# First block, state bank and last rows: six small edits to a hybrid SSD and linear-attention layer

## The chip, the cores and the metric

The kernel runs on one core of one Trainium2 chip. The metric is the device time of one execution in microseconds (us); the median of three executions is compared.

## The reference, cut to what matters

One layer over 2048 real tokens and 16 meta tokens put in front of them, all in float32, width 1024:

```python
u = rmsnorm(hres, norm_w)
proj = jnp.einsum('bld,dn->bln', u, w_in)
z, xbc, dt_raw, q, k, v, g_gla, a_lr, merge_g = split_cols(proj, IN_WIDTHS)
# branch 1: conv + silu of xbc, state-space scan in chunks of 128; 16 heads in 4 groups
# branch 2: gated linear attention; log gates = log_sigmoid(a_lr @ w2 + b) / 16, summed along time; 4 heads
# both states start from the 16 meta tokens
branch_proj = jnp.einsum('blnc,ncd->blnd', branches, w_branch)
gates = jax.nn.sigmoid(merge_g.reshape(b, l, N_BRANCH, D_MODEL))
merged = jnp.sum(gates * branch_proj, axis=2)
return hres + jnp.einsum('bld,de->ble', merged, w_out)     # then a last rmsnorm; meta rows dropped
```

## The kernel before, in words

Each float32 operand of a large product is split into a high and a low half, and TensorE (PE) makes three products of the halves (`accum`, L214 to L216). ScalarE (ACT) makes the high half by a copy, VectorE (DVE) or GpSimd (POOL) the low half by a subtraction. For weights this is `load_w` (L175 on ACT, L177 on POOL) and `load_half` (L189, L190); the tile is `whl`, four buffers, its raw load `wr`, three.

The first part goes over four blocks of 512 tokens; block 0 also holds the meta tokens, and in the code `m0` is then 16, else 0. `load_u(b)` normalizes the block: per slice `kt` of 128 channels DVE scales (L342), ACT writes the high half (L345) and issues a store of the slice to memory (`u_left`, L346), DVE writes the low half (L347). For block 0 this happens at the very start, and the first product, `proj_zm`, goes through eight weight pieces `zm_0` to `zm_7`, in pairs, as the slices appear.

Within a block, generators are advanced by `step()`, once after each piece of the projections that PE works through; each `yield` is a step. The order on PE and on the queue of SyncE (SP) is the order of the code; on ACT, DVE and POOL a scheduler orders the instructions when the kernel is built, and each engine runs its list strictly in order. `gates(o)` makes the log gates of the four heads as two pairs: four small products (L488), each drained by DVE (L490) and ACT (L491), then Exp and Ln on ACT (L493, L494); the running sums (L498, L500, DVE) of each head are put off to the end of a step in block 0. Beside it `proj_conv` drains a projection on ACT (L593, L594), convolves on DVE (L598, three times), takes Tanh on ACT (L601), and `ssd_scan` works on one chunk a step (L662 to L700).

PSUM pools: `pj` (three banks) for projections, `pt` (three) for turns and small products, `pc` (two) for scans. In `gla_scan` of block 0 the state after the meta tokens is one product into a bank (L881), copied by DVE (L882), between products of `level_out` (L848) that use `pc`.

The second part (gates, two branches, output) runs as stages of products of sums (Strassen-Winograd); `sum_a(n)` makes three sums and a difference of an A operand on POOL, and `todo` holds at which position of the product order each step is written. The output stage scales finished rows: `use` takes the squares on ACT (L1251), POOL the power -1/2 (L1261, L1276), `finish` scales the two halves of a row (ACT L1283, DVE L1285 or L1287) and queues two stores, which go out from ACT's queue after the next product (L1377), or at the very end from SP's (L1432).

Of the kernel before, what the change touches and what calls it, by code (L numbers as in the profile page):

```python
# [43 lines left out]
def trunk_kernel(ctx: ExitStack, tc: tile.TileContext, xm, xmt, w_feat, w_tok, w_v3, w_zm, w_br, w_o,  # L44
                 cf32, cmsk, pvec, fnw, hvec, gw2, out):
    nc = tc.nc
# [85 lines left out]
    def bank(pool, tag):  # L132
        return mk(pool, [P, 512], F32, tag)
# [136 lines left out]
    def load_u(b):  # L270
        m0 = META if b == 0 else 0
        row0 = META - m0 + b * BLK
        tt = m0 + BLK
        u = []

        def rows_load(r0, n, i=None):
            xt = mk(wk, [P, D], F32, "tok4", bufs=NT4) if i is None else mk(spool, [P, META + BLK], F32, "acc")[:, :BLK]
            nc.sync.dma_start(xt[:n], xm[r0:r0 + n, :] if i is None else xm[r0:r0 + n, i * BLK:(i + 1) * BLK])
            return xt

        def rstd_rows(ss, n):
            r = mk(sm, [P, 1], F32, "rs1")
            nc.vector.tensor_scalar(r[:n], ss[:n], 1.0 / D, EPS, op0=ALU.mult, op1=ALU.add)
            done = nc.gpsimd.tensor_tensor(r[:n], r[:n], mhalf[:n, 0:1], op=ALU.pow)
            return (r, done) if m0 else r

        def rows_rstd(r0, n, vector):
            ss = mk(sm, [P, 1], F32, "ss")
            xt = rows_load(r0, n)
            if vector:  # L290
                nc.vector.scalar_tensor_tensor(xt[:n], xt[:n], 1.0, xt[:n], op0=ALU.mult, op1=ALU.mult,
                                               accum_out=ss[:n])
            else:
                nc.scalar.activation(xt[:n], xt[:n], AF.Square, accum_out=ss[:n])
            return rstd_rows(ss, n)

        rs = []
        if m0:
            rm_s = rows_rstd(0, META, True)
            for c in range(NCH):  # L300
                rs.append(rows_rstd(META + b * BLK + c * P, P, c % 2))
        else:
            for c in range(NCH):
                s2 = mk(sm, [P, 2], F32, "ss2")
                for i in range(2):
                    xt = rows_load(META + b * BLK + c * P, P, i)
                    nc.scalar.activation(xt, xt, AF.Square, accum_out=s2[:, i:i + 1])
                    if i == 0:
                        yield
                ss = mk(sm, [P, 1], F32, "ss")  # L310
                nc.vector.tensor_tensor(ss, s2[:, 0:1], s2[:, 1:2], op=ALU.add)
                rs.append(rstd_rows(ss, P))
                yield
        if m0:
            rs.append(rm_s)
            first_rows.append(rs[NCH - 1][1])
            rs = [r for r, _ in rs]
            nc.sync.dma_start(cst[:, :2], cf32[:, :2])
            nc.sync.dma_start(pv, pvec)
            for q in range(NWR):  # L320
                raws[f"zm_{q}"] = load_raw(w_zm[:, q * 288:(q + 1) * 288])
        rb = bank(pt, "pt")
        for c in range(NCH):
            nc.tensor.matmul(rb[:, c * P:(c + 1) * P], rs[c].to_broadcast([P, P]), ident, start=True, stop=True)
        rbs = [(rb, m0, BLK)]
        if m0:
            rm = bank(pt, "pt")
            nc.tensor.matmul(rm[:, :META], rs[NCH][:META].to_broadcast([META, P]), ident[:META, :META],
                             start=True, stop=True)
            rbs = [(rm, 0, META)] + rbs  # L330
        else:
            rbc = mk(spool, [P, 3 + META + BLK], F32, "cin")[:, :BLK]
            nc.scalar.activation(rbc, rb, AF.Copy)
            rbs = [(rbc, 0, BLK)]
            yield
        lows = []
        for kt in range(KT):
            xk = (mk(wk, [P, META + BLK], F32, "act", bufs=NACT) if m0 else mk(spool, [P, META + BLK], F32, "acc"))[:, :tt]
            nc.sync.dma_start(xk, xmt[:, kt, row0:row0 + tt])
            with tc.issue_after(lows[kt - 2].ins) if m0 and kt > 1 else nullcontext():  # L340
                for ps, a, n in rbs:
                    nc.vector.scalar_tensor_tensor(xk[:, a:a + n], xk[:, a:a + n], norm_w[:, kt:kt + 1], ps[:, :n],  # L342
                                                   op0=ALU.mult, op1=ALU.mult)
            u.append(u_tile(b)[:, :, :tt])
            nc.scalar.activation(u[kt][:, 0], xk, AF.Copy)  # L345
            nc.scalar.dma_start(u_left[b][kt], xk[:, m0:])  # L346
            lows.append(nc.vector.tensor_tensor(u[kt][:, 1], xk, u[kt][:, 0].bitcast(F32), op=ALU.subtract))  # L347
            if m0:
                first_low[:] = lows[:2][-1:]
            yield  # L350
        return u
# [116 lines left out]
    def gates(o):  # L468
# [12 lines left out]
        for h2 in range(0, GH, 2):  # L481
            gmt = mk(wk, [P, 2, META + BLK], F32, "tok4", bufs=NT4)
            for h in (h2, h2 + 1):
                gm = gmt[:, h % 2, :tt]
                gb = gate_b[:, h:h + 1]
                for i, (a, n) in enumerate(o.segs_all):
                    ps = bank(*((pj, "pj") if m0 and i == 0 else (pt, "pt")))
                    nc.tensor.matmul(ps[:, :n], w2[:, h * P:(h + 1) * P], ast[:, a:a + n],  # L488
                                     start=True, stop=True)
                    nc.vector.tensor_scalar(gm[:, a:a + n], ps[:, :n], gb, 0.0, op0=ALU.add, op1=ALU.min)  # L490
                    evicted[:] = [nc.scalar.activation(g_all[:, h, a:a + n], ps[:, :n], AF.Abs, bias=gb)]  # L491
            ga = g_all[:, h2:h2 + 2, :tt]
            nc.scalar.activation(ga, ga, AF.Exp, scale=-1.0)  # L493
            nc.scalar.activation(ga, ga, AF.Ln, bias=1.0)  # L494
            yield
            for h in (h2, h2 + 1):
                def sums(h=h):
                    nc.vector.tensor_tensor(gmt[:, h % 2, :tt], gmt[:, h % 2, :tt], g_all[:, h, :tt], op=ALU.subtract)  # L498
                    for a, n in chunks:
                        nc.vector.tensor_tensor_scan(g_all[:, h, a:a + n], ones[:, :n], gmt[:, h % 2, a:a + n], 0.0,  # L500
                                                     op0=ALU.mult, op1=ALU.add)

                if m0:
                    put_off.append(sums)
                else:
                    sums()
                yield


# [276 lines left out]
    def gla_scan(o, h, last=False):  # L786
# [90 lines left out]
        level_in(16)  # L877
        yield
        if m0:
            ps = bank(pc, "pc")  # L880
            nc.tensor.matmul(ps[:, :256], btm[:META], s_gla[:META, h], start=True, stop=True)  # L881
            nc.vector.tensor_copy(s_gla[:, h], ps[:, :256])  # L882
        level_out(32)
# [339 lines left out]
                         "p (k c) -> p k c", c=P), fetch, use)  # L1223

    def out_stage():
        fns, res, ssq, at_once = [], {}, {}, []

        def fetch(n, i, t):
            r0 = (2 * n + i) * P
# [7 lines left out]
        def use(n, i, t, ps, snap, cols=None):  # L1237
# [10 lines left out]
            c = cols or slice(0, BLK)  # L1248
            k = t + (c.start > 0)
            latest[:] = [nc.vector.scalar_tensor_tensor(r[:, c], ps[:, c], 0.5, r[:, c], op0=ALU.mult, op1=ALU.add)]  # L1250
            nc.scalar.activation(jk[:, c], r[:, c], AF.Square, accum_out=q[:, k:k + 1])  # L1251
            row = n, i, t
            if row == at_once[-1] or (first and (n, i) in [w[:2] for w in at_once[1:]]):
                if k < 2:
                    nc.vector.tensor_tensor(r[:, c], r[:, c], fns[t][:, c], op=ALU.mult)
                if k == 1 and not first:
                    mean(q)
                if k == 2:
                    last = nc.vector.scalar_tensor_tensor(q[:, 0:1], q[:, 2:3], 1.0 / D, q[:, 0:1],
                                                          op0=ALU.mult, op1=ALU.add)  # L1260
                    nc.gpsimd.tensor_tensor(q[:, 0:1], q[:, 0:1], mhalf[:, 0:1], op=ALU.pow)  # L1261
                    with tc.issue_after(last.ins):
                        nc.vector.tensor_tensor(r[:, c], r[:, c], fns[t][:, c], op=ALU.mult)
                    finish(*row)
            elif row in at_once:
                scale(*row)
                finish(*row)

        def mean(q):
            nc.vector.tensor_tensor(q[:, 0:1], q[:, 0:1], q[:, 1:2], op=ALU.add)  # L1270
# [63 lines left out]
        pos = max(pos, -1)  # L1334
        todo.setdefault(int(pos // 1), []).append((pos, fn))

    def load_sum_a(st, n):
        st.load_a(n)
        st.sum_a(n)

    for i, (st, n, p) in enumerate(order):
        if p == 1 and i >= NEARLY:
            at(i - LOAD + (n % 2), lambda st=st, n=n: load_sum_a(st, n))
    for si, st in enumerate(stages):
        for q in range(0 if si else 12, 28):
            p, j = PS[q // 4], q % 4
# [75 lines left out]
    for i, (st, n, p) in enumerate(order):  # L1422
# [5 lines left out]
            st.product(n, p)  # L1428
            flush(due)
        run(i)  # L1430
    for dst, src in stores:
        nc.sync.dma_start(dst, src)  # L1432
    run_out.close()


# [85 lines left out]
```

## Time and profile before

| what | value |
|---|---|
| three executions, us | 2244.68, 2245.72, 2250.13 (median 2245.72) |
| the profiled execution's own time, us | 2246.09 |
| its span (first to last instruction), us | 2244.0 |
| PE busy | 99% of the span |
| DVE, ACT, POOL busy | 70%, 53%, 31% |

Times in the profile's rows count from the start of the span; the profiled execution is 2.09 us longer than its span. A row of the timeline has the start, the length, the engine, line, operation, `out<-in` and a count (rows that follow each other are merged); in brackets stands how long the engine was idle before, and what ended that. ACTq and SPq are the queues' issues of transfers. A row of waits has engine and tile, what it waited for, and total, times and longest in us.

### The profile page before, as it was taken

What the parts mean: (1) busy time and instruction counts of PE and PEld (TensorE: products, weight loads), DVE (VectorE), ACT (ScalarE), POOL (GpSimd) and SP (SyncE); (2) the same over time, 40 slices, a digit from 0 to 9 for tenths busy, and PEclk for the clock granted to TensorE, in tenths of its full rate; (3) what the DMA queues carried; (4) which work ended last, traced back from release to release, by engine and by line L of the source; (5) the groups of instructions that cost most, each with busy time, mean ns of one, the idle gap of its engine ahead of it and who ended that gap; (6) DMA issues with size and microseconds to landing.
All of it is one profiled execution on the core that took longest, in us unless ns stands there. A gap on an engine that the chain in (4) does not pass through costs nothing.

```text
span 2244.0 us, 34943 instructions
## 1 busy us (share of the span) xinstructions
PE 2213.1 (99%) x11789; PEld 1896.7 (85%) x11789; DVE 1574.2 (70%) x2935; ACT 1188.8 (53%) x2767; POOL 688.1 (31%) x681
## 2 busy tenths in 40 slices
PE   7999999999999999999999999999999999999998
PEld 7999999888888888888988888878888888888887
DVE  5786676677657676557577666675678954789876
ACT  5666654476445456545465454454644545454544
POOL 4344433222222122221123100076233374324341
PEclk9999999999999999999999999999999999999999
DMA  8767876767778667778667664386768866677753
GB/s 310 237 226 237 267 257 213 220 207 248 240 250 267 205 215 236 240 250 268 208 219 226 212 216 157 125 260 200 242 220 292 303 221 216 239 281 249 254 178 123
DMA packets 314210, 517.94 MB, mean 231 GB/s; under 512 B 28080, under 2 KB 162480, under 8 KB 314032
## 3 DMA queue, kind: packets, MB, share of 16 engines
q1 hardware_dynamic: 246864, 419.63, 58.1%
q10 hardware_dynamic: 67168, 96.10, 11.8%
q8 instruction: 92, 1.51, 0.3%
q14 instruction: 86, 0.70, 0.1%
HBM read 368.42 MB, written 147.19 MB: 230 GB/s over the span
## 4 chain that ended last, share of the span: by engine, by line
PE 90%; DVE 3%; DMA 3%; ACT 2%; issue 1%; SPq 0%; POOL 0%; POOLq 0%; ACTq 0%; DVEq 0%
PE pj L214 20%; PE pj L216 20%; PE pj L215 20%; PE pt L214 4%; PE pt L215 4%; PE pt L216 4%; PE pc L687 2%; PE pc L214 2%; PE pc L216 2%; PE pc L215 2%; PE pc L848 2%; PE pc L688 1%; PE pc L690 1%; PE pc L956 1%; PE pt L662 1%
## 5 line engine op out<-in xcount | busy, mean ns | idle before, releaser
L214 PE MATMUL pj<-ue,whl 128*128 128x264 f32 (+1 forms) x672 | 236.3, 352 | 3.1 <-ACT g_all L491 2.2
L216 PE MATMUL pj<-ue,whl 128*128 128x264 f32 (+1 forms) x672 | 230.4, 343 | 0.0
L215 PE MATMUL pj<-ue,whl 128*128 128x264 f32 (+1 forms) x672 | 229.5, 342 | 0.0
L214 PE MATMUL pj<-uo,whl 128*128 128x512 f32 x512 | 205.7, 402 | 0.0
L216 PE MATMUL pj<-uo,whl 128*128 128x512 f32 x512 | 200.1, 391 | 0.0
L215 PE MATMUL pj<-uo,whl 128*128 128x512 f32 x512 | 199.4, 389 | 0.0
L215 PE MATMUL pj<-b,a 128*128 128x512 f32 (+1 forms) x484 | 188.0, 388 | 2.2 <-DVE b L1107 2.1
L214 PE MATMUL pj<-b,a 128*128 128x512 f32 (+1 forms) x484 | 188.7, 391 | 0.7 <-DVE io L1250 0.5
L216 PE MATMUL pj<-b,a 128*128 128x512 f32 (+1 forms) x484 | 188.9, 390 | 0.0
L598 DVE SCALAR_TENSOR_TENSOR acc<-cin,hcw,acc 128x512 f32<-128x512 f32 (+1 forms) x192 | 155.5, 810 | 41.6 <-ACT acc L594 40.3
L83 POOL TENSOR_TENSOR wr<-wr 128x256 f32<-128x256 f32 x80 | 67.9, 848 | 375.0 <-DMA wr<-y 160.1
L1132 DVE TENSOR_TENSOR a<-ar,a 128x512 fp32r<-128x512 f32 x160 | 132.8, 837 | 63.3 <-ACT a L1131 60.5
L1122 POOL TENSOR_TENSOR as<-ar,ar 128x512 f32<-128x512 f32 x40 | 63.0, 1575 | 370.3 <-DMA ar<-in_w_br 140.0
L1107 DVE TENSOR_TENSOR b<-br,b 128x512 fp32r<-128x512 f32 x140 | 128.7, 941 | 23.3 <-ACT b L1106 22.4
L214 PEld LDWEIGHTS pj<-ue,whl 128*128 128x128 f32 x672 | 127.0, 189 | 19.4 <-ACT g_all L491 2.4
L216 PEld LDWEIGHTS pj<-ue,whl 128*128 128x128 f32 x672 | 127.1, 189 | 14.9
L215 PEld LDWEIGHTS pj<-ue,whl 128*128 128x128 f32 x672 | 127.1, 189 | 14.7
L177 POOL TENSOR_TENSOR whl<-wr,whl 128x512 fp32r<-128x512 f32 (+1 forms) x76 | 97.8, 1294 | 131.0 <-ACT whl L175 73.6
L1132 DVE TENSOR_TENSOR a<-as,a 128x512 fp32r<-128x512 f32 x120 | 105.7, 882 | 42.5 <-ACT a L1131 39.8
L1166 ACT ACTIVATE sn<-pj 128x512 f32<-128x512 f32 x118 | 69.8, 592 | 122.6 <-PE pj L216 71.7
L1131 ACT ACTIVATE a<-ar 128x512 fp32r<-128x512 f32 x160 | 99.0, 624 | 56.4 <-PE pt L216 24.7
L215 PE MATMUL pt<-b,a 128*128 128x512 f32 x320 | 125.4, 392 | 0.1
(328 smaller groups left out, 6448.4 us busy)
## 6 DMA issues: line engine op xcount, KB each, us to landing
whl<-k_s SPq DMA_DIRECT2D x96, 512.0 KB, 3.7
whl<-k_g SPq DMA_DIRECT2D x96, 512.0 KB, 4.3
whl<-k_v SPq DMA_DIRECT2D x36, 512.0 KB, 4.0
wr<-in_w_feat SPq DMA_DIRECT2D x64, 256.0 KB, 4.5
k_s<-whl SPq DMA_DIRECT2D x32, 512.0 KB, 3.7
cb<-cumd SPq DMA_DIRECT2D x64, 256.0 KB, 5.0
y<-gg ACTq DMA_DIRECT2D x64, 256.0 KB, 4.0
k_g<-whl SPq DMA_DIRECT2D x32, 512.0 KB, 3.9
```

The lines of the kernel that those rows point to most:

```text
L83: nc.gpsimd.tensor_tensor(o, x, y, op=ALU.subtract)
L177: nc.gpsimd.tensor_tensor(hl[:, 1], raw, hl[:, 0].bitcast(F32), op=ALU.subtract)
L214: nc.tensor.matmul(ps, sh, mh, start=first, stop=False, **kw)
L215: nc.tensor.matmul(ps, sh, ml, start=False, stop=False, **kw)
L216: nc.tensor.matmul(ps, sl, mh, start=False, stop=last, **kw)
L598: convd[:] = [nc.vector.scalar_tensor_tensor(acc, cin[:, k:k + tt], hcw[:, ti, k:k + 1], acc, op0=ALU.mult, op1=ALU.add)]
L687: nc.tensor.matmul(py[:, h * 64:(h + 1) * 64], dm[:, h], xdt[:, h], start=True, stop=True)
L1107: nc.vector.tensor_tensor(t[:, 1], raw, t[:, 0].bitcast(F32), op=ALU.subtract)
L1122: nc.gpsimd.tensor_tensor(s1, a21, a22, op=ALU.add)
L1131: nc.scalar.activation(t[:, 0], src, AF.Copy)
L1132: latest[:] = [nc.vector.tensor_tensor(t[:, 1], src, t[:, 0].bitcast(F32), op=ALU.subtract)]
L1166: nc.scalar.activation(sn, self.ps[n, "a"], AF.Copy)
```

## The change

Six edits. (1) In block 0 the eight stores of `u_left` are issued from GpSimd's queue in place of ACT's. (2) In `gates` of block 0 one more `yield` follows the first pair of heads, so that the second pair's products come one step later. (3) The meta state of `gla_scan` takes a bank of `pt` in place of `pc`. (4) In the output stage, `finish` of the last row but one is called inside the last row's last `use`, behind its last square, and (5) the stores left at the end are reordered: the last row's later half goes from SP's queue ahead of its earlier half, which goes from ACT's. (6) `sum_a` is written three positions behind `load_a` for the first 28 positions.

```diff
-            nc.scalar.dma_start(u_left[b][kt], xk[:, m0:])
+            (nc.gpsimd if m0 else nc.scalar).dma_start(u_left[b][kt], xk[:, m0:])
...
                     sums()
                 yield
+            if m0 and not h2:
+                yield
...
         if m0:
-            ps = bank(pc, "pc")
+            ps = bank(pt, "pt")
             nc.tensor.matmul(ps[:, :256], btm[:META], s_gla[:META, h], start=True, stop=True)
...
-            nc.scalar.activation(jk[:, c], r[:, c], AF.Square, accum_out=q[:, k:k + 1])
+            squared = nc.scalar.activation(jk[:, c], r[:, c], AF.Square, accum_out=q[:, k:k + 1])
...
                 if k == 2:
+                    with tc.issue_after(squared.ins):
+                        finish(*unfinished.pop())
                     last = nc.vector.scalar_tensor_tensor(q[:, 0:1], q[:, 2:3], 1.0 / D, q[:, 0:1],
...
                 scale(*row)
-                finish(*row)
+                if row == at_once[-2]:
+                    unfinished.append(row)
+                else:
+                    finish(*row)
...
-            at(i - LOAD + (n % 2), lambda st=st, n=n: load_sum_a(st, n))
+            pos = i - LOAD + (n % 2)
+            at(pos, lambda st=st, n=n: st.load_a(n))
+            at(pos + (3 if i < 28 else 0), lambda st=st, n=n: st.sum_a(n))
...
-    for dst, src in stores:
-        nc.sync.dma_start(dst, src)
+    early, late = stores[-2:]
+    for (dst, src), q in zip(stores[:-2] + [late, early], [nc.sync] * (len(stores) - 1) + [nc.scalar]):
+        q.dma_start(dst, src)
```

**Edit 1, POOL at the start.** POOL's list before, from the third low half of the `zm` weights (`whl_443`) to the seventh (`whl_528`):

```order
L177 TENSOR_TENSOR whl_443<-wr_300,whl_443 128x288
L177 TENSOR_TENSOR whl_447<-wr_449,whl_447 128x288
L177 TENSOR_TENSOR whl_484<-wr_486,whl_484 128x288
L177 TENSOR_TENSOR whl_491<-wr_493,whl_491 128x288
L177 TENSOR_TENSOR whl_528<-wr_530,whl_528 128x288
```

And of the changed kernel, at the same place (`u_0` to `u_6` are the slices' stores):

```order
L177 TENSOR_TENSOR whl_443<-wr_300,whl_443 128x288
L346 DMA u_0_64<-act_309 128x512
L346 DMA u_1_65<-act_317 128x512
L346 DMA u_2_66<-act_325 128x512
L346 DMA u_3_67<-act_333 128x512
L346 DMA u_4_68<-act_341 128x512
L177 TENSOR_TENSOR whl_447<-wr_449,whl_447 128x288
L346 DMA u_5_69<-act_349 128x512
L177 TENSOR_TENSOR whl_484<-wr_486,whl_484 128x288
L346 DMA u_6_70<-act_357 128x512
L177 TENSOR_TENSOR whl_491<-wr_493,whl_491 128x288
```

Five stores now stand ahead of the fourth weight piece, and one between each of the next. On ACT the same stores stood between the high halves (L345) and are gone.

**Edit 2, PE at the second gate pair.** PE's list before, from the end of one convolution feature (`whl_1389`) to the start of the next (`whl_1492`):

```order
L216 MATMUL pj_1357<-ue_369,whl_1389 128x264
L488 MATMUL pj_1435<-act_1005,w_387 128x264
L488 MATMUL pt_1439<-act_1005,w_387 128x264
L488 MATMUL pj_1443<-act_1005,w_387 128x264
L488 MATMUL pt_1447<-act_1005,w_387 128x264
L662 MATMUL pt_1455<-cst,act_682 128x128
L662 MATMUL pt_1455<-cst,act_772 128x128
L662 MATMUL pt_1455<-cst,act_858 128x128
L687 MATMUL pc_1475<-c_161_1321,sq_1328 128x64 x4
L688 MATMUL pc_1475<-s_ssd,act_936 128x256
L690 MATMUL pc_1481<-c_162_1323,bt_1326 128x256
L214 MATMUL pj_1490<-ue_313,whl_1492 128x264
```

The changed kernel, from the same feature's end (its lines are two higher from there on: L664 is L662 of before):

```order
L216 MATMUL pj_1357<-ue_369,whl_1389 128x264
L664 MATMUL pt_1436<-cst,act_682 128x128
L664 MATMUL pt_1436<-cst,act_772 128x128
L664 MATMUL pt_1436<-cst,act_858 128x128
L689 MATMUL pc_1456<-c_161_1321,sq_1328 128x64 x4
L690 MATMUL pc_1456<-s_ssd,act_936 128x256
L692 MATMUL pc_1462<-c_162_1323,bt_1326 128x256
L214 MATMUL pj_1471<-ue_313,whl_1473 128x264
```

The four products L488 are gone from here; they stand behind the next feature, ahead of the next chunk. On ACT, the drains of that next feature (`pj_1471`) now stand behind the Tanh of the feature before it (`act_1431`; L603 and L595, L596 are L601 and L593, L594 of before):

```order
L679 ACTIVATE sq_1447<-sq_1447 128x512
L603 ACTIVATE act_1431<-acc_1421 128x528
L593 ACTIVATE cin_1874<-tails 128x3
L189 ACTIVATE whl_1690<-wr_1692 128x512
L595 ACTIVATE cin_1535<-pj_1471 128x264
L596 ACTIVATE acc_1536<-pj_1471,hcb,hcw 128x264
```

The drains keep their place behind that Tanh; what follows the feature on PE is now the second gate pair, and its third product takes the bank that this L596 leaves.

More of the change, by code (lines that the diff above doesn't have):

```diff
@@ L1225, in out_stage @@
     def out_stage():
-        fns, res, ssq, at_once = [], {}, {}, []
+        fns, res, ssq, at_once, unfinished = [], {}, {}, [], []
         def fetch(n, i, t):
@@ L1335, in at @@
         todo.setdefault(int(pos // 1), []).append((pos, fn))
-    def load_sum_a(st, n):
-        st.load_a(n)
-        st.sum_a(n)
     for i, (st, n, p) in enumerate(order):
         if p == 1 and i >= NEARLY:
-            at(i - LOAD + (n % 2), lambda st=st, n=n: load_sum_a(st, n))
+            pos = i - LOAD + (n % 2)
+            at(pos, lambda st=st, n=n: st.load_a(n))
+            at(pos + (3 if i < 28 else 0), lambda st=st, n=n: st.sum_a(n))
     for si, st in enumerate(stages):
```

## The prediction

> **What bounds the kernel now.** I read the page first, then who waited for whom on PE, then the timeline where those waits lie. The page:
>
> ```profile
> PE 2213.1 (99%) x11789; PEld 1896.7 (85%) x11789; DVE 1574.2 (70%) x2935; ACT 1188.8 (53%) x2767; POOL 688.1 (31%) x681
> ```
>
> PE bounds it. No product is added or taken away, so what the change can give is what PE loses in waits, and the tail behind its last product. PE's waits (total, times, longest):
>
> ```profile
> PE pt L324 <- DMA cst<-in_cf: 10.0, 1, 10.0
> PE pj L214 <- ACT ue L345: 2.4, 2, 1.5
> PE pj L214 <- ACT g_all L491: 2.2, 1, 2.2
> PE pc L848 <- DVE s_gla L882: 0.8, 1, 0.8
> PE pc L687 <- DVE sq L678: 0.8, 1, 0.8
> PE pj L488 <- ACT acc L594: 0.6, 1, 0.6
> PE pt L446 <- DVE ecu L443: 0.6, 1, 0.6
> PE pc L646 <- DVE c L698: 0.3, 1, 0.3
> PE pj L214 <- ACT alr L428: 0.2, 1, 0.2
> ```
>
> The first is the wait for the first rows, which no edit touches. All others that the edits touch come to some 7 us of 2244. A measurement of this kernel tells about 0.3%, 6.7 us, from no change; so the answer depends on small terms.
>
> **Edit 1, the start.** ACT's queue before:
>
> ```profile
> 12.90 1.55 DVE L342 SCALAR_TENSOR_TENSOR act<-act,pv,pt 128x512 f32<-128x512 f32 x3 [0.73 <-PE pt L324]
> 14.98 0.89 DVE L342 SCALAR_TENSOR_TENSOR act<-act,pv,pt 128x16 f32<-128x16 f32 x2
> 15.45 0.35 ACTq L346 DMA_DIRECT2D u<-act  x1
> 15.90 0.64 ACT L345 ACTIVATE ue<-act 128x528 fp32r<-128x528 f32 x1 [1.58 <-DVE act L342]
> 16.58 0.71 DVE L347 TENSOR_TENSOR ue<-act,ue 128x528 fp32r<-128x528 f32 x1 [0.71 <-ACT ue L345]
> 17.34 0.61 PE L216 MATMUL pj<-whl,ue 128*128 128x288 f32 x1
> ```
>
> DVE had scaled slice 1 at 12.90 + 1.55 = 14.45, yet ACT began its high half at 15.90: the store of slice 0 stood in front and got out only at 15.45. Without it ACT is done at 14.45 + 0.64 = 15.1. DVE then makes the low half right behind its next two scalings, at 14.98 + 0.89 = 15.87, and it is ready at 15.87 + 0.71 = 16.6, less the overlap that successive DVE rows show (0.1). PE's L216 of slice 1 goes at 16.5 in place of 17.34: 0.82 gained.
>
> The price lies on POOL, which makes the low halves of the weights:
>
> ```profile
> 11.59 2.29 POOL L177 TENSOR_TENSOR whl<-wr,whl 128x288 fp32r<-128x288 f32 x3
> 18.73 1.02 SPq L203 DMA_DIRECT2D wr<-in_w_zm  x1
> 21.27 1.33 POOL L177 TENSOR_TENSOR whl<-wr,whl 128x288 fp32r<-128x288 f32 x1 [7.38 <-DMA wr<-in_w_zm]
> 23.54 0.30 PE L215 MATMUL pj<-whl,ue 128*128 128x288 f32 x1
> 27.38 0.30 PE L215 MATMUL pj<-whl,ue 128*128 128x288 f32 x1
> ```
>
> POOL is free at 13.88, and PE first needs the fourth piece's low half (the row at 21.27) at 23.54, by my gain at 22.7. Five stores stand in between. If one costs x on POOL, the piece is ready at 13.88 + 5x + 1.33, in time while x is below 1.5. No trace of before has a DMA on POOL. The nearest rows are an issue on ACT (0.35) and SP (1.02) and a POOL instruction (1.33); I take 1.1, between the latter two and nearer to the issue, which is the same kind of work. The stores wait for their slices too: at a scaling and a low half a slice (0.89 + 0.71) slice 4 comes from DVE at 14.98 + 2 x 1.6 + 0.89 = 19.1, so the fifth store ends at 20.2 and the piece is ready at 21.5, in time. The later stores stand one between two pieces, where POOL waits for ACT's high half; that wait hides them. A gain on POOL is excluded, since it only gets work.
>
> [...] No run here shows a POOL DMA yet.
>
> ACT, freed of eight issues, also runs ahead later. The copy that frees the bank (L428) moves ahead of a weight split, and so does the head of the dt chain, which had stood behind this one:
>
> ```profile
> 38.01 0.63 ACT L175 ACTIVATE whl<-wr 128x512 fp32r<-128x512 f32 x1 [2.29 <-DMA k_s<-whl]
> ```
>
> That takes away the waits of 0.2 (alr) and 0.6 (ecu). Start: 0.8 + 0.2 + 0.6 = 1.6 gained.
>
> **Edit 2, the second gate pair.** Before:
>
> ```profile
> 90.62 0.47 PE L214 MATMUL pj<-ue,whl 128*128 128x264 f32 x1
> 95.80 0.65 ACT L601 ACTIVATE act<-acc 128x528 f32<-128x528 f32 x1 [2.69 <-DVE acc L598]
> 96.72 0.39 PE L488 MATMUL pj<-act,w 48*128 48x264 f32 x1
> 97.24 0.56 ACT L594 ACTIVATE acc<-pj,hcb,hcw 128x264 f32<-128x264 f32 x1
> 97.85 0.39 PE L488 MATMUL pj<-act,w 48*128 48x264 f32 x1 [0.62 <-ACT acc L594]
> 97.86 3.98 DVE L500 TENSOR_TENSOR_SCAN g_all<-ones_r,tok 128x16 f32<-128x16 f32 x5
> 100.24 0.47 PE L214 MATMUL pj<-ue,whl 128*128 128x264 f32 x1
> 103.13 0.39 PE L214 MATMUL pj<-ue,whl 128*128 128x264 f32 x1 [2.16 <-ACT g_all L491]
> 103.68 0.75 DVE L598 SCALAR_TENSOR_TENSOR acc<-cin,hcw,acc 128x528 f32<-128x528 f32 x1
> 107.02 0.76 DVE L598 SCALAR_TENSOR_TENSOR acc<-cin,hcw,acc 128x528 f32<-128x528 f32 x1
> 104.40:107.70 3.30, 3.30 (x18) 3.30 (x17) 3.30 (x10) 3.28 (x10) 0.00 (x0) 0.52 0.18 50
> ```
>
> DVE's running sums of the first pair (to 101.84) hold the drains of the second pair; PE waits 2.16, and then, the last row says, runs 3.3 us at a granted clock of 0.52, another 3.3 x 0.48 = 1.6 lost. Now the pair comes a feature later. That feature starts without the four products, 97.85 to 100.24 less their own half us, at 98.7, and takes what the one before took, 90.62 to 96.72: the pair's first product is due at 104.8, the third at 105.3. The third needs the bank that ACT drains (L594), and on ACT that stands behind Tanh L601 of the feature before. That one waits for DVE's convolution, which stands behind the same running sums: free at about 102.1, nine instructions that took 103.68 to 107.78 before, done at 106.2. From L601 to the first L594 ACT took 95.80 to 97.80, 2.0 us: the bank is free at 108.2. So the stall does not go, it moves: 2.9 us on L488, for 0.6 + 2.2 before. Behind the third product the rest is as before (2.4 us), so the z projection starts at 110.6 and not, as before, 1.5 us later, clock loss included; if the low clock comes again (the longer stall makes that likely) 1.5 - 1.6 = -0.1. The waits on L678 (0.8) and L698 (0.3) go, since the Ln and the sums leave that step. Edit 2: 1.0 gained, 2.6 without low clock.
>
> [...]
>
> **The rest.** Edit 3 takes the state's copy off the two `pc` banks, so the next products no longer wait for it: the 0.8 goes. A bank of `pt` is one more in use of three; its last reader there is a copy on ACT that ended while PE ran the projection in between, so it costs nothing; were that cover gone, the wait would be again at most the copy's own 0.8. Edit 6 does not do what it says: no row of any engine's list moves by it, POOL's four sums stand where they stood, so it is nothing. Edits 4 and 5, the tail:
>
> ```profile
> 2237.07 0.72 ACT L1283 ACTIVATE io<-io,ssf 128x512 f32<-128x512 f32 x1 [1.18 <-POOL ssf L1276]
> 2237.26 0.74 DVE L1287 SCALAR_TENSOR_TENSOR io<-io,ssf,br 128x512 f32<-128x512 f32 x1
> 2237.70 0.40 ACT L1251 ACTIVATE junk<-io 128x256 bf16<-128x256 f32 x1
> 2238.23 0.16 DVE L1259 SCALAR_TENSOR_TENSOR ssf<-ssf 128x1 f32<-128x1 f32 x1 [0.22 <-ACT junk L1251]
> 2239.91 0.82 SPq L1432 DMA_DIRECT2D out_h<-io  x2
> ```
>
> The last square no longer stands behind a scaling of 0.72; it could go 0.3 earlier, but DVE's next step stays behind L1287, which ends at 2238.0: 0.2. Of two stores one after the other on SP (0.82) each queue has one: 0.4. The row before's two stores, now ahead of the last on SP, are issued before it is due. Tail: 0.6.
>
> Sum: 1.6 + 1.0 + 0.8 + 0.6 = 4.0 us. Against the profiled execution's own 2246.09 that is 2242.1; the median of the runs shown lies 0.4 lower, so I forecast 2241.7 for the median.
>
> **The rivals.** *The stall goes altogether.* The sums' 3.98 us are long: ten of the same took 2.79 later, five 1.4. Two of POOL's splits (L190) ran beside the long ones:
>
> ```profile
> 123.59 2.79 DVE L500 TENSOR_TENSOR_SCAN g_all<-ones_r,tok 128x16 f32<-128x16 f32 x10
> ```
>
> If the second split falls behind the sums (on ACT its high half now stands behind L675), DVE is 2.6 us earlier, the new stall is 0.3, and 0.6 + 2.2 + 1.6 + 0.8 + 0.3 less 0.3 = 5.2 are won in place of 1.0: 8.2 in all, 2237.5. Against it: another split, that of the piece before, stays beside the sums. Chance 0.24.
>
> *POOL's stores cost more*; this one ends slower than before. If each store takes a POOL instruction's 1.33 and is held by the DVE pair beside it (0.89), x is 2.22: the fourth piece is ready at 13.88 + 11.1 + 1.33 = 26.3, 3.6 late; two more stores and pieces (2 x 3.55) later the sixth comes at 33.4, and PE, which needed it at 27.38, wants it at 27.38 - 0.8 + 3.6 = 30.2: 3.2 more. The start pays 6.8 against its gain of 1.6; with the other edits' 2.4 that is 6.8 - 1.6 - 2.4 = 2.8 slower, 2248.5. It decides from x = 1.5. For it: the same subtraction took 1.33 with DVE at work, and 2.29 for three of them without much of it. Chance 0.12, a third of it past 0.3%, for an x nearer to 3. [...]
>
> *The start's lead is eaten.* From 20 to 40 us the DMA engines are full:
>
> ```profile
> 20.00:40.00 20.00, 19.76 (x147) 19.55 (x146) 10.23 (x24) 9.89 (x26) 8.97 (x8) 1.00 0.97 330
> ```
>
> If the weights' loads pace PE as soon as it is earlier, the 1.6 go and 2.4 stay: 2243.3. Against it: no wait of PE there names a weight. Chance 0.16.
>
> **How the numbers follow.** The forecast itself has 0.48. Its own bounds are 2240.1 (no low clock) and 2243.3. The range takes in the first rival and the third and stops short of the second's 2248.5: 2236.5 to 2247.0; less than 0.2 is left out. Faster by over 0.3% (below 2239.0) is the first rival and 0.02 of the forecast's edge: 0.26. Slower by that (above 2252.4): 0.04. The rest, 0.70, is within.
>
> **What would show it.** Right: L216 of slice 1 near 16.5; POOL's DMA rows near 1.1 us and no wait of PE on a `whl`; PE's wait on g_all gone, one of 2 to 3 us on L488 behind L596, with a clock row near 0.5 behind it; no wait on s_gla; the last two issues side by side, 0.6 earlier. Wrong: a wait on L177, or no wait at all at the second pair.

## The result

The changed kernel takes 2243.57 us (median of 21 runs, 2239.68 to 2246.45), the kernel before 2246.85 (21 runs, 2244.68 to 2251.68): a ratio of 0.9984, 95% interval 0.9978 to 0.9990. It is faster by 3.3 us by the medians, 2.2 to 4.9 by the interval. Forecast were 2241.7 and a gain of 4.0, in a range of 2236.5 to 2247.0.

The changed kernel's profiled execution took 2246.45, the longest of its 21, with a span of 2244.7. So the two spans can't be subtracted; I compare stretch by stretch. PE runs the same 11,789 products, so the start of one product, counted from PE's first, says how far ahead PE is there. The page's row of PE, then PE's waits (total, times, longest):

```profile
PE 2211.9 (99%) x11789; PEld 1896.8 (85%) x11789; DVE 1577.0 (70%) x2935; ACT 1187.0 (53%) x2767; POOL 693.9 (31%) x689
PE pt L215 <- DVE b L1109: 3.9, 3, 1.7
PE pj L488 <- ACT acc L596: 3.1, 1, 3.1
PE pc L214 <- DVE c L946: 1.9, 4, 0.6
PE pj L214 <- ACT ue L345: 1.5, 1, 1.5
PE pj L214 <- ACT acc L596: 1.2, 2, 1.1
PE pt L446 <- DVE ecu L443: 1.0, 1, 1.0
PE pj L214 <- ACT alr L428: 0.6, 1, 0.6
```

Gone are the waits on s_gla, g_all, sq, tok and the c of L698, and that on ecu at 41.7 us (the 1.0 here lies at 768). New are 3.1 on L488, as forecast, and 1.1 on acc, which was not. The wait on alr, which was to go, grew from 0.2 to 0.6. The 3.9 on b lies at 1477 to 1484, far from any edit.

The start, POOL's queue and the product of slice 1 on PE:

```profile
14.07 1.35 POOL L346 DMA_DIRECT2D u<-act  x2
16.28 0.54 POOL L346 DMA_DIRECT2D u<-act  x1 [0.86 <-DVE act L342]
20.24 0.80 POOL L177 TENSOR_TENSOR whl<-wr,whl 128x288 fp32r<-128x288 f32 x1 [0.26 <-ACT whl L175]
20.98 0.56 POOL L346 DMA_DIRECT2D u<-act  x1
16.65 0.61 PE L216 MATMUL pj<-whl,ue 128*128 128x288 f32 x1 [0.33 <-DVE ue L347]
```

L216 goes at 16.65 where it went at 17.34. The first two stores take POOL 1.35 together, each later one 0.54 to 0.56, and the fourth piece is ready at 21.04.

The second gate pair, stretches of 3.4 us (length, busy time and count of PE, PEld, DVE, ACT, POOL, then PE's granted clock, DMA share, GB/s):

```profile
103.20:106.60 3.40, 1.24 (x9) 0.88 (x7) 3.40 (x8) 1.23 (x4) 0.00 (x0) 0.99 0.61 202
106.60:110.00 3.40, 2.42 (x11) 2.19 (x11) 3.39 (x7) 3.40 (x10) 2.85 (x3) 0.50 0.07 26
110.00:113.40 3.40, 3.40 (x13) 3.04 (x13) 3.23 (x8) 3.40 (x10) 1.24 (x2) 0.50 0.97 317
113.40:116.80 3.40, 3.40 (x31) 3.40 (x30) 3.04 (x6) 2.78 (x5) 0.00 (x0) 1.00 0.41 125
```

PE stands still, then has half its clock (0.50) for two such stretches; DVE is full through the first two. That row of DVE, not PE's, is the one to read here.

The last stores: issues in the timeline, then the issues of the last few stores with their time to landing (us at the end of the row), of the changed kernel and, last row, of the kernel before:

```profile
2239.29 1.31 SPq L1438 DMA_DIRECT2D out_h<-io  x3
2240.37 0.34 ACTq L1438 DMA_DIRECT2D out_h<-io  x1
out_h<-io SPq DMA_DIRECT2D x1, 256.0 KB, 2.5
out_h<-io ACTq DMA_DIRECT2D x1, 256.0 KB, 3.0
...
out_h<-io SPq DMA_DIRECT2D x1, 256.0 KB, 2.3
```

The table shows how far ahead (minus) or behind PE is at the same product, against the kernel before's profile, at times of that profile. "ch." is the changed kernel.

| kernel | 20 us | 52 | 60 | 96 | 140 | 400 | 425 | 1450 | 2236 |
|---|---|---|---|---|---|---|---|---|---|
| ch. | -0.80 | -1.75 | -0.88 | -0.82 | -1.70 | -2.38 | -3.46 | -1.12 | +0.58 |
| ch. again | -0.97 | -3.17 | -2.39 | -2.01 | -4.00 | -4.72 | -5.69 | -3.94 | -4.51 |
| edit 1 alone | -0.99 | -1.19 | -0.41 | -0.40 | -0.51 | -0.72 | -0.94 | -0.37 | 0.00 |
| edit 2 alone | -0.58 | -0.74 | -0.72 | -0.70 | -2.63 | -2.87 | -3.08 | -3.13 | -2.62 |
| ch. without 2 | -0.80 | -2.22 | -1.44 | -1.10 | -1.14 | -1.70 | -2.78 | -2.60 | -3.21 |
| edits 3 to 6 | -0.52 | -0.35 | -0.36 | -0.03 | +2.07 | +1.39 | +0.31 | +1.19 | +0.36 |
| ch. without 5 | -1.00 | -3.55 | -2.55 | -2.55 | -3.66 | -4.32 | -5.40 | -2.13 | -0.58 |
| ch., 48-row filler | -0.80 | -2.19 | -1.41 | -1.41 | -1.83 | -2.33 | -3.41 | -1.10 | -1.22 |
| ch., split moved | -0.81 | -2.73 | -2.47 | -2.47 | -2.90 | -3.64 | -4.72 | -3.46 | -3.35 |
| ch., two steps | -0.81 | -2.74 | -1.95 | -1.24 | -4.43 | -5.22 | -6.35 | -4.93 | -5.68 |
| ch., 128-row filler | -0.80 | -2.34 | -1.56 | -0.93 | -2.64 | -3.32 | -4.40 | -2.68 | -0.94 |
| two steps, split, old tail | -0.80 | -2.21 | -1.96 | -1.38 | +0.08 | -0.67 | -1.80 | -0.98 | -0.03 |
| the same, three steps | -0.81 | -2.78 | -2.44 | -1.51 | -0.69 | +1.92 | +0.84 | +2.22 | +2.12 |

A single row is one execution, and where no edit is, executions of like kernels differ by up to 3 us (the columns 425 and 1450); what a column does in all rows with an edit, and in none without, is the edit's.

### The profile page after: what moved, and what is told of

It reads as the page before. It is cut to its first block, busy times and chain, and to the rows that moved or that the text cites. A ratio compares the mean times of both kernels' runs of the same rounds, so it can differ in the third digit from the quotient of the medians.

```text
span 2244.7 us, 34971 instructions
## 1 busy us (share of the span) xinstructions
PE 2211.9 (99%) x11789; PEld 1896.8 (85%) x11789; DVE 1577.0 (70%) x2935; ACT 1187.0 (53%) x2767; POOL 693.9 (31%) x689
## 3 DMA queue, kind: packets, MB, share of 16 engines
q8 instruction: 92, 1.51, 0.3%
## 4 chain that ended last, share of the span: by engine, by line
PE 89%; DVE 4%; DMA 3%; ACT 2%; issue 1%; POOL 1%; SPq 0%; POOLq 0%; ACTq 0%; DVEq 0%
PE pj L214 20%; PE pj L216 20%; PE pj L215 19%; PE pt L215 4%; PE pt L214 4%; PE pt L216 4%; PE pc L689 2%; PE pc L214 2%; PE pc L216 2%; PE pc L215 2%; PE pc L850 2%; PE pc L690 1%; DMA acc<-in_xmt 1%; PE pc L692 1%; PE pc L958 1%
## 5 line engine op out<-in xcount | busy, mean ns | idle before, releaser
L216 PE MATMUL pj<-ue,whl 128*128 128x264 f32 (+1 forms) x672 | 229.7, 342 | 0.0
L216 PE MATMUL pj<-uo,whl 128*128 128x512 f32 x512 | 200.1, 391 | 0.0
L216 PE MATMUL pj<-b,a 128*128 128x512 f32 (+1 forms) x484 | 188.9, 390 | 0.3 <-DVE a L1134 0.3
L216 PEld LDWEIGHTS pj<-ue,whl 128*128 128x128 f32 x672 | 126.4, 188 | 14.9
```

The source lines that it names most:

```text
L216: nc.tensor.matmul(ps, sl, mh, start=False, stop=last, **kw)
```

## The experiments

The experiments ran in three groups of four, each beside its own 33 runs of the kernel before (medians 2246.21, 2245.85 and 2246.04). A ratio is against those, so kernels of different groups are compared by their ratios.

**The edits one by one.** Edit 1 alone:

```diff
-            nc.scalar.dma_start(u_left[b][kt], xk[:, m0:])
+            (nc.gpsimd if m0 else nc.scalar).dma_start(u_left[b][kt], xk[:, m0:])
```

> The kernel before with edit 1 alone (u's left stores from GpSimd's queue). I measure how much earlier PE does the same product than in the kernel before, counted from PE's first product. Theory (the start's lead is won at once and half of it is spent by 56 us): 0.8 us earlier at 20 us, 1.1 at 28, 1.6 behind the wait on ecu (45 us), then a wait of about 1.1 us on acc at 55, which leaves 0.9 at 60; nothing of the later waits moves, so the whole run is 0.9 us shorter. Rival A: the wait on acc at 55 us belongs to edit 2 and not to this one; then 1.6 to 1.75 stay at 60 and to the end. Rival B (POOL's stores cost): a wait on a whl low half (L177) between 20 and 30 us and less than 0.3 left at 45.

Measured: 2244.73 against 2246.21 for before, ratio 0.9990 (0.9981 to 0.9999). PE's wait on acc is there (1.0), so it belongs to edit 1: rival A falls. The lead grew to 1.59 at 28 us but was lost to weight pieces between 30 and 32 us (0.9 behind ACT's high half of whl and 0.5 behind POOL's low half, after 0.3 behind another low half at 22), a part of rival B. POOL's issues are not the cause: ACT itself waited 3.59 for the load of the piece at 30 us, 1.34 for the same one in the changed kernel's profile, and no other profile with edit 1 has those waits. So in this execution the weights came late. That is the rival "the start's lead is eaten", in one execution of eleven.

Edit 2 alone:

```diff
+            if m0 and not h2:
+                yield
```

> The kernel before with edit 2 alone (one step more between the two gate pairs). Theory: the waits of 0.6 at 97.85 and 2.2 at 103.13 go, one of 3.1 us on L488 at about 108 comes, with a clock row at half speed behind it for about 6.8 us in place of 3.4; the waits on sq, c and tok between 118 and 130 (0.8, 0.3, 0.2) go; together PE is 0.9 us earlier at 140 us than in the kernel before, and the run 0.9 us shorter. Rival (the low clock's length is chance, not a result of where the stall lies): the stall as said, but 3.4 us of half clock, and 2.4 or more earlier at 140 us. Rival (the start's lead of edit 1 is what removes the waits between 118 and 130): those waits stay, and PE is 0.4 us later at 140 than before.

Measured: 2245.41, ratio 0.9994 (0.9985 to 1.0003). From 96 to 140 us PE gains 1.93, with one stretch of half clock of 3.4 us; the waits on sq, c and tok are gone without the start's lead, so they go by edit 2 and the last rival falls. The length of the half clock differs from one execution to the next, as the first rival says (6.8 and 3.4 us in the two profiles of the changed kernel), though the gain stayed below its 2.4. PE's waits of this kernel and, second pair of rows, of edit 1 alone:

```profile
PE pj L488 <- ACT acc L596: 3.2, 1, 3.2
PE pc L850 <- DVE s_gla L884: 0.6, 1, 0.6
...
PE pj L214 <- ACT g_all L491: 2.1, 1, 2.1
PE pc L687 <- DVE sq L678: 2.0, 1, 2.0
```

The second pair matters. In this execution without edit 2 PE stood 2.1 us at g_all and no half clock followed, yet PE came out no earlier: the wait on sq, 0.8 in the profile before, was 2.0.

The changed kernel without edit 2:

```diff
-            if m0 and not h2:
-                yield
```

> The changed kernel without edit 2. Theory: PE keeps the 0.9 us that the start leaves at 60 us through 140 us, with the waits of 0.6 and 2.2 us at the second gate pair back and 3.4 us of half clock; state bank 0.8 to 1.1 at 425; tail nothing; in all 1.7 to 2.0 us shorter than before, that is 0.9 us slower than the changed kernel. Rival (the parts don't add): with the start's lead but without the step the stall on g_all grows by what the lead gave, and at 140 us nothing is left: 0.8 to 1.1 shorter than before in all.

Measured: 2243.56, ratio 0.9989 (0.9981 to 0.9998). From 96 to 140 us it gains 0.04; the waits are 0.6, 2.1 and 2.0, with no half clock. The start and the bank are won, as the theory says, and the stall on g_all did not grow. By time it is no slower than the changed kernel: 0.9 us is less than these medians tell.

Edits 3 to 6, that is the changed kernel without those two lines and with

```diff
-            (nc.gpsimd if m0 else nc.scalar).dma_start(u_left[b][kt], xk[:, m0:])
+            nc.scalar.dma_start(u_left[b][kt], xk[:, m0:])
```

> The kernel before with edits 3 to 6 (state bank, tail, sums) and neither 1 nor 2. Theory: no difference up to 300 us; the wait on s_gla at 421.75 gone, 0.8 us earlier behind it; the tail from PE's last wait (2235.20 before) to the last landing as long as before (7.4 us; the pair of queues gives nothing, since the store on ACT's queue lands 3.0 us after its issue beside three on SP's where it took 2.1 before): 0.8 us shorter in all. Rival (my forecast): the tail is 0.6 us shorter, 1.4 in all. For the waits on b between 1470 and 1492 (2.1 us in the profile before, 4.2 in the changed one): if edits 3 to 6 make them, they are near 4 here; if they vary from one execution to the next, anything from 2 to 4.

Measured: 2245.83, ratio 0.9996 (0.9987 to 1.0005). The wait on s_gla is gone and PE gains 1.08 between 400 and 425 us; with nothing changed there, edits 1 and 2 alone show 0.2. The tail from PE's last wait to the last landing is 7.48 us, as the theory says and not as I forecast. The waits on b were 2.0. From 96 to 140 us, where this kernel has no edit, PE loses 2.1 in this execution: it waits 2.0 on sq, and the clock is halved for 6.8 us behind it.

**The tail.** The changed kernel without edit 5:

```diff
-    early, late = stores[-2:]
-    for (dst, src), q in zip(stores[:-2] + [late, early], [nc.sync] * (len(stores) - 1) + [nc.scalar]):
-        q.dma_start(dst, src)
+    for dst, src in stores:
+        nc.sync.dma_start(dst, src)
```

> The changed kernel without edit 5: the last stores all on SP in their old order, edit 4 kept. The tail is counted from PE's last wait (L214 behind io, 2235.20 before, 2235.91 changed) to the last landing: 7.41 us before, 7.48 changed. Theory (edit 4 wins 0.25 and the store on ACT's queue, which takes 3.0 us to land where SP's took 2.3, gives it back): 7.15 to 7.25 here, the whole 0.25 us shorter than the changed kernel. Rival (the stores of the row before, which edit 4 puts behind the last square, crowd the last ones on SP's queue): 7.5 or more, since now all four stand on one queue. My forecast's terms would make it 7.4 less 0.2 here and 0.4 more in the changed kernel.

Measured: 2242.25, ratio 0.9984 (0.9975 to 0.9993); tail 7.46. So edit 4 alone, without the second queue, already uses up what the earlier last steps win, as in the rival, but not by crowding SP's queue: with one queue or two the tail is the same. The GB/s rows of the DMA view between 2239 and 2244 us, 40 slices of 0.125 us, first the kernel before, then the changed one:

```profile
GB/s 410 344 443 328 426 344 410 377 164 0 0 0 0 16 344 328 426 344 442 361 393 344 426 360 344 66 0 0 0 0 0 0 0 0 0 0 0 0 0 0
GB/s 0 0 0 0 0 0 0 0 0 360 344 410 344 459 295 393 377 442 344 377 394 344 442 344 426 311 426 344 410 377 328 99 0 0 0 0 0 0 0 0
```

Before, the stores of the row but one end at 2240.1, before the last two start. In the changed kernel all four run in one piece from 2240.1 to 2243.0 at the same 380 GB/s or so: four stores of 256 KB are 1.05 MB, 2.8 us at that rate, and the second queue did not make it shorter. The last store was issued earlier, by 0.68 counted from PE's last wait, and took 3.0 us to land in place of 2.3. The two stores of the row but one, which edit 4 holds back, were issued 0.76 and 0.72 later than before. Edit 5 without edit 4 was not run. In seven profiles with edits 4 and 5 the tail was 7.47 to 7.49 (7.84 in the eighth), in five with neither 7.40 or 7.41.

**The wait on acc.** ACT's timeline of the kernel before at 53 us, then of the changed one with PE's product:

```profile
52.65 0.63 ACT L189 ACTIVATE whl<-wr 128x512 fp32r<-128x512 f32 x1 [1.25 <-PE pj L216]
53.79 0.65 ACT L601 ACTIVATE act<-acc 128x528 f32<-128x528 f32 x1 [0.50 <-DVE acc L598]
55.43 0.56 ACT L594 ACTIVATE acc<-pj,hcb,hcw 128x264 f32<-128x264 f32 x1
...
53.15 0.65 ACT L603 ACTIVATE act<-acc 128x528 f32<-128x528 f32 x1 [2.01 <-DVE acc L600]
53.80 0.62 ACT L189 ACTIVATE whl<-wr 128x512 fp32r<-128x512 f32 x1
54.68 0.56 ACT L596 ACTIVATE acc<-pj,hcb,hcw 128x264 f32<-128x264 f32 x1
55.30 0.39 PE L214 MATMUL pj<-ue,whl 128*128 128x264 f32 x1 [1.09 <-ACT acc L596]
```

With the stores gone from ACT's list, the scheduler put the weight split L189 behind the Tanh in place of ahead of it, right in front of the drain for which PE waits. Moved behind the drains (`third` is the drain of the third feature):

```diff
+        with tc.issue_after(third.pop().ins) if third else nullcontext():
+            nc.scalar.activation(hl[:, 0], raw, AF.Copy)
```

> The changed kernel with one weight split on ACT (the first piece of the z projection, 0.62) put behind the drains of the third feature at 55 us, in front of which edit 1 had moved it. Theory (that split makes the wait of 1.0 to 1.1 on acc that all kernels with edit 1 show and none without): the wait is 0.2 to 0.4, and the lead that PE has at 52 us over the kernel before stays to 60 us but for 0.1; 0.75 us shorter in all. Rival (the split is then late for its own product at 61 us, a wait on whl between 60 and 64): nothing won or some tenths lost. Rival (PE's lead makes the wait, since ACT can't be earlier): a wait of about 1 us stays.

Measured: 2242.18, ratio 0.9983 (0.9974 to 0.9992). The wait is 0.5:

```profile
53.12 0.56 ACT L597 ACTIVATE acc<-pj,hcb,hcw 128x264 f32<-128x264 f32 x1
53.73 0.39 PE L215 MATMUL pj<-ue,whl 128*128 128x264 f32 x1 [0.50 <-ACT acc L597]
54.30 1.16 ACT L190 ACTIVATE whl<-wr 128x512 fp32r<-128x512 f32 x2
```

From 52 to 60 us PE loses 0.26 where the eight profiles with edit 1 and the split left alone lost 0.78 to 1.00 and the three without edit 1 at most 0.02. So the split in front of the drain makes some 0.5 of the wait; in the two later kernels with the same move the loss is 0.25 and 0.34. What is left of it is not settled.

**The half clock.** The changed kernel, with the second of the second pair's products computed 13 times:

```diff
+                    for _ in range(13 if m0 and h2 and h == h2 and i else 1):
```

> The changed kernel with the second of the second gate pair's four products computed 13 times over into the same bank (same result), some 2.8 us of PE's work in its wait of 3.1 us. [...] Rival (the half clock is not tied to idling): a clock row at 0.5 behind 106 us all the same.

Measured: 2243.53, ratio 0.9989 (0.9980 to 0.9997). Twelve products of 48 rows took only 1.5 us of the wait, 1.6 stayed, and the clock was halved for 6.8 us all the same, as the last rival says. With 24 products of 128 rows:

```diff
+                    for _ in range(24 if m0 and h2 and h == h2 and i else 0):
+                        nc.tensor.matmul(ps[:, :n], o.u[0][:, 0, :P], o.u[1][:, 0, a:a + n], start=True, stop=True)
```

> The changed kernel with 24 products of 128 rows (u's first two slices) into the bank of the second of the second gate pair's products, ahead of it, which overwrites them: 2.9 us of PE's work in its wait of 3.1. The twelve of 48 rows before took only 1.5 of it and the clock fell all the same. Theory (the clock falls when PE does little in a window, and DVE sets the time there): the wait on L488 is 0.5 or less, no row at half speed near 108, the mean clock is 0.999 in most executions where the changed kernel had 0.998 or 0.997 in 19 of 21; yet the median is within 0.8 us of the changed kernel's on this chip. Rival (the half clock costs PE's time): 1.5 us or more shorter than the changed kernel. Rival (the fall is not tied to PE's work): mean clocks as in the changed kernel.

Measured: 2245.18, ratio 0.9996 (0.9987 to 1.0005). The same stretches as above:

```profile
103.20:106.60 3.40, 3.40 (x27) 3.12 (x26) 3.40 (x9) 1.23 (x4) 0.00 (x0) 1.00 0.81 277
106.60:110.00 3.40, 3.40 (x26) 3.04 (x25) 2.85 (x6) 2.75 (x7) 2.94 (x3) 1.00 0.02 5
110.00:113.40 3.40, 3.40 (x29) 3.35 (x28) 3.40 (x7) 1.56 (x5) 1.60 (x2) 1.00 0.95 313
113.40:116.80 3.40, 2.80 (x24) 2.60 (x22) 3.06 (x8) 3.40 (x11) 0.00 (x0) 1.00 0.47 149
```

PE is never idle at the pair, the clock stays whole, and over all executions the mean clock is 0.999 in 9 of 11, against 2 of 21 for the changed kernel and 1 of 11 when it ran again in this group. So the fall of the clock follows PE's idling there, and it can be bought off. It won nothing: PE gains 1.7 from 96 to 140 us, as two executions of one half-clock stretch did without filler (1.9 and 2.0), since the wait on DVE's sq is back (1.6): DVE, busy for 13.06 of these 13.6 us in the changed kernel, sets the time there. A second stretch does cost: executions with two gained 0.4 to 1.1. In the same group the changed kernel took 2241.63, 3.5 us less than the filled one, where I had expected at most 0.8 between them. The two profiles are 1.3 apart at 425 and at 1450 us and 3.6 at 2236, with waits on b of 3.9 and 2.1 in between. Why the filled kernel is slower stays open.

**More steps.** Two steps between the pairs:

```diff
             if m0 and not h2:
                 yield
+                yield
```

> The changed kernel with two steps between the gate pairs in place of one. Theory (PE waits there because it runs ahead of DVE, which has no gap from 88 to 116 us; a step later DVE has caught up a little, so the wait shrinks): a wait of 1 to 2.5 us on L488 in place of 3.1, at 115 to 125 us, so that a clock window at half speed is rarer; up to 1 us shorter than the changed kernel. Rival (the backlog is the same wherever it is met): a wait of 3 us a step later; same time within 0.3. Rival (the pair's sums now meet the next group's scan): waits on sq, c or tok behind 118 us of 1 us or more; 1 us slower.

Measured: 2241.11, ratio 0.9981 (0.9972 to 0.9990). L488 waits 1.1, but sq 2.1 at 106: both the theory and the last rival in part. PE gained 3.2 from 96 to 140 us, in an execution without a half clock.

What seemed to help, together: the kernel before with

```diff
+            (nc.gpsimd if m0 else nc.scalar).dma_start(u_left[b][kt], xk[:, m0:])
...
+            if m0 and not h2:
+                yield
+                yield
...
+            ps = bank(pt, "pt")
...
+        with tc.issue_after(third.pop().ins) if third else nullcontext():
+            nc.scalar.activation(hl[:, 0], raw, AF.Copy)
```

> What the runs so far speak for, together: edits 1 and 3, two steps between the gate pairs, the weight split behind the drains at 55 us, and the tail of before (no edit 4, 5, 6). Theory (the parts add): two steps won 1.9 over one by PE's place at 140 us, the split 0.6, the old tail 0.08: 2.5 us shorter than the changed kernel, 5.5 to 6 shorter than before. Rival (PE's lead is given back where POOL's sums hold DVE's small steps, at 700 to 800 us and at 1475 to 1490): 1 to 1.5 shorter than the changed kernel.

Measured: 2242.84, ratio 0.9979 (0.9971 to 0.9988). The parts don't add. The same two steps cost 1.5 here from 96 to 140 us: the waits are alike (2.1 and 1.0), but in this execution the clock was halved behind each, for 6.8 and 3.4 us. So what two steps gain differs from one execution to the next, and this kernel can't be told from the changed one.

And with one more:

```diff
                 yield
                 yield
+                yield
```

> As the last but one, with three steps between the gate pairs. Theory (the second pair's own work on DVE only moves; with two steps there were waits of 2.1 on sq at 106 and 1.1 on g_all at 115): the 1.1 shrinks or moves behind 120 us, within 0.7 us of two steps. Rival (the pair's sums come too late for the first head's gates, which need all heads' sums): a wait of 2 us or more on g_all or tok between 125 and 160 us, 1 to 3 us longer.

Measured: 2243.76, ratio 0.9989 (0.9980 to 0.9998). The rival holds only in part: there are waits of 1.0 on tok at 133 (it said 2 or more) and, not named by it, of 1.5 on sq at 160 us. At 425 us PE is 2.6 us behind the last kernel in these two executions; by the medians it is 0.9 us longer, which the intervals don't tell apart.

The changed kernel again, with no edit:

> The changed kernel once more, beside the others on the same chip and with a profile of its own. Theory (the waits on b between 1475 and 1490, 4.2 us in its first profile, vary from one execution to the next, as those at 700 to 800 do): 1.5 to 4 us there, and the wait of 1.0 on acc at 55 us and of 3.1 on L488 at 107 as before; tail 7.48. Rival (they belong to the change): 3.5 us or more again.

Measured: 2241.63, ratio 0.9981 (0.9972 to 0.9990). The waits on acc (1.0) and on L488 (3.1) are there, those on b are 2.1 in place of 3.9, and there is one stretch of half clock. So the waits on b vary. No kernel run here beats the changed one by more than its interval.

## Why the prediction was right

Edits 2 and 3 did what was forecast, but for the price of a half clock. Edit 1 came near its number by errors that offset each other, and edits 4 and 5 won nothing.

**Edit 1: 1.6 forecast, 1.2 measured, by two errors.** L216 came where I put it (16.65, in an execution that began 0.12 later than before's), but most of that 0.8 hangs on the one execution of the kernel before. With edit 2 alone, which changes nothing at the start, ACT's store of slice 0 went out 0.6 earlier than in the profile before (its times count from a start 0.05 earlier):

```profile
14.82 0.34 ACTq L346 DMA_DIRECT2D u<-act  x1
15.96 0.61 PE L214 MATMUL pj<-whl,ue 128*128 128x288 f32 x1 [0.29 <-ACT ue L345]
16.70 0.61 PE L216 MATMUL pj<-whl,ue 128*128 128x288 f32 x1
```

So L216 came 0.58 earlier there without the edit, and 0.52 with edits 3 to 6; against those two the edit wins 0.2 to 0.3 at this place. Its gain comes later. Profiles with edit 1 are 2.4 ahead at 52 us in the mean of eleven, those without 0.4, the kernel before among them: 2.1 won, more than forecast. By 40 us it is 1.0 (means of 1.5 and 0.5); the rest is the wait on ecu, which goes in all eleven and is 0.6, 0.9 and 0.7 in the three without edit 1, and what follows it. The wait on alr, forecast to go, is there in three of the eleven (0.6, 0.3 and 0.2). Then 0.8 are given back to acc at 55 us: means of 1.6 and 0.4 at 60 us over the eight profiles that leave the split alone and the three without edit 1. The step that failed is "ACT, freed of eight issues, also runs ahead later": I read from the order what moved ahead, up to the dt chain, and not what moved behind, some twenty rows further on. POOL's price, taken as 1.1, was 0.5 to 0.7 on average, so the second rival's point at 1.5 was far off. No run shows an x nearer to 3, for which a third of that rival's chance stood: in the changed kernel's profile POOL's issues took 0.54 to 0.56, and 1.35 for the first two together, with DVE at work through all of them, scaling and subtracting. The stores land later, a median of 5.1 us after the issue where ACT's took 4.1, and PE waits for none of them; why they land later is not known.

**Edit 2: 1.0 forecast, 1.3 measured**, the mean of the five profiles with one step and no filler (0.4 to 2.0 from 96 to 140 us), against 0.1 and 0.0 in the two without it that kept the clock whole (edit 1 alone, and the changed kernel without edit 2). The place, the size (2.9 forecast, 3.1) and the low clock were as forecast. The price that I put on before's half clock, 1.6, was wrong: the two profiles without it wait 2.0 on sq in place of 0.8 and come out only those 0.1 and 0.0 earlier, so its 3.4 us cost some 0.1 in these executions. A longer half clock does cost: with edits 3 to 6 it lasted 6.8 us and PE lost 2.1. Against the mean of all four profiles without edit 2 the edit would be worth 1.8, so the 1.3 hangs on which executions were profiled. What edit 2 wins is the waits on sq, c and tok behind the pair, 0.8 + 0.3 + 0.2 in the profile before. My rival that the second split makes the stall go altogether was not borne out.

**Edit 3: 0.8 forecast, 0.9 measured** (1.08, less the mean of 0.14 in the three profiles without it).

**Edits 4 and 5: 0.6 forecast, 0.1 lost.** Both terms held up to the issue: ACT's and DVE's last steps came 0.26 earlier, the last issue 0.68. The step that failed is "issued before it is due" of the row before's two stores: issued they were, but 0.7 later than in the kernel before, and their bytes stood in front of the last ones' on the DMA engines.

**Edit 6: nothing**, by the order alone: POOL's list with edits 3 to 6 is that of the kernel before. It had no run of its own.

Sum: 1.2 + 1.3 + 0.9 - 0.1 = 3.3, against 3.3 by the medians. That the two agree is luck: between 425 and 1450 us, where no edit is, profiles with edit 1 lose 1.5 in the mean (0.2 to 3.3) and those without it 0.3, and with this 1.2 taken off the sum is 2.1. By the medians of their own runs edit 1, edit 2 and edits 3 to 6 win 1.5, 0.8 and 0.4, of which only the first is clear of no gain. One piece of the loss is plain. DVE's small steps and POOL's sums of the changed kernel at 766 us, then of the kernel before:

```profile
765.71 1.04 DVE L905 TENSOR_TENSOR c<-c,act 128x128 f32<-128x128 f32 x2 [1.56 <-ACT c L902]
767.74 0.74 DVE L443 TENSOR_TENSOR ecu<-tkd,nega 128x64 f32<-128x64 f32 x1
765.83 1.64 POOL L83 TENSOR_TENSOR wr<-wr,wr 128x256 f32<-128x256 f32 x2
768.54 0.43 PE L446 MATMUL pt<-ecu,cst 128*128 128x64 f32 x2 [1.04 <-DVE ecu L443]
...
767.87 0.49 DVE L903 TENSOR_TENSOR c<-c,act 128x128 f32<-128x128 f32 x2 [1.56 <-ACT c L900]
769.35 0.21 DVE L443 TENSOR_TENSOR ecu<-tkd,nega 128x64 f32<-128x64 f32 x1
```

The same steps take 1.04 and 0.74 beside POOL's sums, 0.49 and 0.21 without, and PE waits 1.04. Ten of the eleven profiles with edit 1 had that wait, none of the three without. Their lists are the same there. In the ten, POOL's sums start 3.3 to 3.5 us before that product is due on PE, in the four others 1.1 to 2.7; why they start sooner is not known, and that they slow DVE is read from the overlap alone.

## What to carry to other kernels

Where an edit takes rows out of a scheduled queue, read the order to the end of the region on every engine: what fell behind something counts as much as what moved ahead. Before a stall of the bounding engine is priced, look which engine is full through it (here DVE, 13.06 of 13.6 us); if another one is, a faster clock or a filled wait can come back as the next wait, as the 2.0 and the 1.6 on sq did here. The last four stores here were bounded by bytes once they ran together (some 380 GB/s, from one queue or two), so let the early ones go as soon as they can.

## What the hardware showed

Between PE's first product and its last the half clock (a granted 0.50) came in stretches of 3.4 or 6.8 us, behind waits of 1.0 to 3.2 us, but not behind each: the waits on g_all (2.1) and sq (2.0) had none with edit 1 alone and without edit 2, while that on g_all (2.2) had 3.4 us in the kernel before and that on sq (2.0) 6.8 us with edits 3 to 6, on the same products. Twelve products of 48 rows, which took 1.5 us of a wait of 3.1, did not keep the clock up (6.8 us of half clock); 24 of 128 rows, 3.19 us of PE, did (1.00). Whether by the rows or by the time that they fill isn't told apart here.
